# Hybrid attention layer: the last two row tiles of each projection group computed weight by weight as one

## The chip, the cores and the metric

The kernel runs as one program on one core of a Trainium2 chip. The metric is the device time of one execution in microseconds (us). Before the change the median of three runs was 1129.72 us (1129.55 to 1129.81).

## The reference

One decoder layer over 1024 rows of width 1024, in float32:

```
h = x + W_out( concat[ A heads | B heads ] )      # both read RMSNorm(x) @ W_in
y = h + W_down( relu(W_up @ RMSNorm(h))^2 )
```

- A heads: 8 query heads on 2 key/value heads of 64, a sliding window of 128 in banded blocks (128 queries against up to 256 keys), ALiBi slopes, a sink logit for each head, normalised queries and keys.
- B heads (forgetting attention): 8 heads of 64, causal, with logit[t,s] += c[t] - c[s], where c is the running sum of log sigmoid of a gate; normalised queries and keys.
- The MLP widens to 4096.

Every large product is computed in three passes on a high and a low part of each operand (hi*hi + hi*lo + lo*hi), so one tile of a projection is 8 weight blocks x 3 = 24 matmuls of 128x384 (or 128x392).

## The kernel before, in words

The program has four stages: a first projection (group A0, until 41.3 us), the attention (41.3 to 467.4 us), the up projection and the down projection. The change touches only the attention.

**Projections.** Five groups of 8 row tiles run during the attention: A1 (queries of the A heads, and the gates) and P0 to P3 (queries, keys and values of one pair of B heads each). `load_w` (L203) brings the 8 weight blocks of a group: a DMA into `wr` (3 buffers), a cast to `wh` on ScalarE, a subtraction into `wl` on GpSimd (8 buffers each of `wh` and `wl`). A buffer is free for the next group's block k when the last row tile of the group has used block k. `proj` (L216) computes one row tile into one PSUM bank of the pool `pd`, which has two banks, so that row tiles alternate. A ScalarE copy then empties the bank into `qkb` (L582) or `q` (L415), and after every fourth tile (every second in A1) `qknorm` normalises on GpSimd, VectorE and ScalarE.

**Attention units.** There are 16 A units (2 key/value heads x 8 blocks, `heads_a`) and 32 B units (4 pairs x 2 heads x 4 blocks of 256 queries, `heads_b`). A unit's scores are issued first and its mixing (transposes `tpa`/`tpb`, the split of these into `pth` on ScalarE and `ptl` on VectorE, the products `pv`/`pvb` with the values) two units later (`DEPTH`). Each unit appends its last score matmul to `marks`; "mark n" below is the last score matmul of unit n.

**Order.** Projection tiles, and later the first half of the output projection (`out_first`, matmuls `po`), are fillers: `PACE` says after how many marks each is released, and its first matmuls are put behind that mark on TensorE (`paced`). A scheduler then fixes each engine's order when the program is built: attention work has the higher priority, the splits of weights and the copies out of `pd` the highest. On the chip every engine works through its queue in that order. All loads and stores shown below are issued from SyncE's queue.

**Preparation of the next pair.** `ahead(p, u)` issues, after unit u of the 8 before pair p: at u = 4 the queries (`prep_q`: transposes, ScalarE and VectorE splits into `q1b`), at u = 5 the keys of head 0 (`prep_k`: transposes, two casts `k1b` on ScalarE and a subtraction `k2z` on VectorE for each half, one load of the gate sums `cb`), at u = 6 the values, at u = 7 the keys of head 1.

**Hand-over to the output projection.** `out_start` closes the pools of the projections, opens new ones in their place and loads the mixed heads (`mix`, 1 MB each). So its loads wait for the last projection matmul of P3. `split_mix` (SPLITS) reads a pair's mixed rows back (`mixr`), normalises and splits them; it has one buffer of each kind.

Of the kernel before, what the change touches and what calls it, by code (L numbers as in the profile page):

```python
# [8 lines left out]
F32 = mybir.dt.float32  # L9
# [3 lines left out]
ALU = mybir.AluOpType  # L13
# [3 lines left out]
P = 128  # L17
D = 1024
S = 1024
KT = D // P  # L20
NT = S // P
# [9 lines left out]
HPO = 8000  # L31
HPA = 5000
# [6 lines left out]
ORDER_END = (1, 3, 0, 2)  # L39

PACE = (
# [5 lines left out]
)  # L47

SPLITS = ((0, 4), (0, 7), (1, 1), (1, 4), (1, 6), (2, 5), (3, 5))
# [4 lines left out]
def hybrid_layer(  # L54
# [13 lines left out]
    nc = tc.nc  # L68

    def mm(out, lhsT, rhs, start, stop):  # L70
        return nc.tensor.matmul(out, lhsT, rhs, start=start, stop=stop)  # L71
# [8 lines left out]
    def rsqrt(pool, out, t, shape, tag):  # L80
# [15 lines left out]
        out=ident, in_=ident, pattern=[[-1, P]], compare_op=ALU.not_equal,  # L96
# [10 lines left out]
    ga, gm, vec, bfb, snk = (  # L107
        vt[:, a:b] for a, b in ((0, 8), (8, 16), (16, 20), (20, 28), (28, 36))
    )
# [3 lines left out]
    for i in range(2):  # L113
        nc.vector.tensor_tensor(
            out=gqk[:, i : i + 1], in0=vec[:, 2 * i : 2 * i + 1],
            in1=vec[:, 2 * i + 1 : 2 * i + 2], op=ALU.mult,
# [3 lines left out]
    rstd = cp.tile([P, NT], F32, name="rstd")  # L120
    ep2 = cp.tile([P, NT], F32, name="ep2")
    rqk = cp.tile([P, NT, 6], F32, name="rqk")
# [14 lines left out]
    xh = xg_p.tile([P, KT, S], F32R, name="xh")  # L137
    xl = xg_p.tile([P, KT, S], F32R, name="xl")
# [7 lines left out]
        out=maskd, in_=maskd, pattern=[[-1, P]], compare_op=ALU.is_ge,  # L146
# [21 lines left out]
    for k in range(KT):  # L168
# [6 lines left out]
        for cs in halves:  # L175
            nc.scalar.activation(xh[:, k, cs], xr[:, cs], AF.Copy, scale=ga[:, k : k + 1])
            nc.vector.scalar_tensor_tensor(
                out=xl[:, k, cs], in0=xr[:, cs], scalar=ga[:, k : k + 1],
                in1=xh[:, k, cs].bitcast(F32), op0=ALU.mult, op1=ALU.subtract,
# [21 lines left out]
    pd = psd.enter_context(tc.tile_pool(name="pd", bufs=2, space=PSUM, reuse_waits="tile"))  # L201

    def load_w(src, n):  # L203
        his, los = [], []
        for k in range(KT):
            wr, wh, wl = w_tiles()
            nc.sync.dma_start(wr[:, :n], src[:, k, :])
            with tc.high_priority(offset=HPO):
                split(wh[:, :n], wl[:, :n], wr[:, :n], nc.scalar, nc.gpsimd)
            his.append(wh)  # L210
            los.append(wl)
        return his, los

    middle = []

    def proj(w, n, t):  # L216
        his, los = w
        ps = pd.tile([P, 512], F32, tag="pd", name="ps")
        tsl = slice(t * P, (t + 1) * P)
        for k in range(KT):  # L220
            mm(ps[:, :n], xh[:, k, tsl], his[k][:, :n], k == 0, False)
            mm(ps[:, :n], xh[:, k, tsl], los[k][:, :n], False, False)
            pe = mm(ps[:, :n], xl[:, k, tsl], his[k][:, :n], False, k == KT - 1)
            if k == KT // 2:
                middle.append(pe.ins)
        return ps

    def qknorm(x, nh, tlo, thi, r=None):


        n = thi - tlo
        w = nh * HD
        sq = ap2.tile([P, 1024], F32, tag="sq", name="sq", bufs=1)
        sqv = sq[:, : n * w].rearrange("p (t c) -> p t c", t=n)
        xv = x[:, tlo:thi, :w]
        nc.gpsimd.tensor_tensor(out=sqv, in0=xv, in1=xv, op=ALU.mult)
        ss, r0, u = (
            ap2.tile([P, 16], F32, tag=tag, name=tag, bufs=2)[:, : n * nh]
            for tag in ("ss", "sr0", "su")
        )  # L240
        nc.vector.tensor_reduce(
            out=ss, in_=sq[:, : n * w].rearrange("p (g d) -> p g d", d=HD),
            axis=AX.X, op=ALU.add,
        )
        th = lambda a: a.rearrange("p (t h) -> p t h", h=nh)
        nc.vector.scalar_tensor_tensor(
            out=th(ss), in0=th(ss), scalar=1.0 / HD,
            in1=ep2[:, tlo:thi].unsqueeze(2).to_broadcast([P, n, nh]),
            op0=ALU.mult, op1=ALU.add,
        )  # L250
        nc.scalar.activation(r0, ss, AF.Ln)
        nc.scalar.activation(r0, r0, AF.Exp, scale=-0.5)
        nc.vector.tensor_tensor(out=u, in0=r0, in1=r0, op=ALU.mult)
        nc.vector.tensor_tensor(out=u, in0=u, in1=ss, op=ALU.mult)
        na = nh + (2 if r is not None else 0)
        if r is None:
            rv = ap2.tile([P, 16], F32, tag="r", name="r", bufs=2)[:, : n * nh]
            rv = th(rv)
        else:
            rv = r[:, tlo:thi, :]  # L260
        nc.vector.scalar_tensor_tensor(
            out=rv[:, :, :nh], in0=th(u), scalar=3.0, in1=th(r0),
            op0=ALU.subtract, op1=ALU.mult,
        )
        for t in range(n):
            xt = x[:, tlo + t, : na * HD].rearrange("p (h d) -> p h d", d=HD)
            nc.gpsimd.tensor_tensor(
                out=xt, in0=xt, in1=rv[:, t].unsqueeze(2).to_broadcast([P, na, HD]), op=ALU.mult
            )

    def split_v(src, name):
        v = ap1.tile([P, NT, P], F32R, tag="v", name=name, bufs=2)
        nc.vector.tensor_copy(v[:, :, :HD], src)
        nc.gpsimd.tensor_tensor(
            out=v[:, :, HD:], in0=src, in1=v[:, :, :HD].bitcast(F32), op=ALU.subtract
        )
        return v
# [17 lines left out]
    def paced():  # L295
        return tc.issue_after(marks[-1]) if marks else nullcontext()
# [4 lines left out]
    def tiles_q_a(g, c):  # L301
        for j in range(2):
            qa[g, j, c] = ap2.tile([P, 2, 512], F32R, tag="q1", name=f"q1a{g}{j}", bufs=4)
# [62 lines left out]
    wa1 = load_w(w_a1, 392)  # L366
    rt = cp.tile([P, NT], F32, name="rt")
    for t in range(NT):
# [4 lines left out]
        out=rt, in0=rt, scalar1=1.0 / D, scalar2=EPS, op0=ALU.mult, op1=ALU.add  # L373
# [4 lines left out]
    q3 = qk_t("q3")  # L378
    z = ap2.tile([P, NH, NT], F32, name="z")
    for t in range(0, NT, 4):  # L380
# [8 lines left out]
        out=dist, in_=dist, pattern=[[-1, 256]], compare_op=ALU.is_ge, fill=BIG,  # L389
# [3 lines left out]
        out=dist, in_=dist, pattern=[[1, 256]], compare_op=ALU.is_ge, fill=BIG,  # L393
# [7 lines left out]
    for pattern, base, sign in (  # L401
# [5 lines left out]
            out=before, in_=before, pattern=pattern, compare_op=ALU.is_ge, fill=0.0,  # L407
            base=base, channel_multiplier=sign,
        )

    def wa1_tile(t):
        with paced():
            ps = proj(wa1, 392, t)
        with tc.high_priority(offset=HPA):
            nc.scalar.copy(q3[:, t, :], ps[:, :384])  # L415
            nc.vector.scalar_tensor_tensor(
                out=z[:, :, t], in0=ps[:, 384:392], scalar=rstd[:, t : t + 1], in1=bfb,
                op0=ALU.mult, op1=ALU.add,
            )
            if t % 2:  # L420
                qknorm(q3, 6, t - 1, t + 1)

    def forget_gates():
        zf = z.rearrange("p h t -> p (h t)")
# [39 lines left out]
    def start_a():  # L464
        for c in range(2):
            tiles_q_a(0, c)
        for t in range(2):
            wa1_tile(t)
        for c in range(2):
            wa1_tile(2 + c)  # L470
            with tc.issue_after(middle[-1]):
                prep(make_k_a, q0, P, c)
            prep(make_q_a, 0, c, 0)
        for g in range(2):
            va.append(split_v(q0[:, :, 256 + g * HD : 256 + (g + 1) * HD], f"va{g}"))
        prep(make_q_a, 0, 0, 1)
        for t in range(4, NT):
            wa1_tile(t)
        prep(make_q_a, 0, 1, 1)

    def scores_a(g, i):
# [89 lines left out]
    def project_b(p):  # L571
        got = {}

        def tile_t(t):
            if t == 0:
                got["w"] = load_w(w_b[p], 384)
                qkb[p] = qk_t(f"qkb{p}")
            qk = qkb[p]
            with paced():
                ps = proj(got["w"], 384, t)  # L580
            with tc.high_priority(offset=HPO):
                nc.scalar.copy(qk[:, t, :], ps[:, :384])  # L582
            if t % 4 == 3:
                with tc.high_priority(offset=HPA):
                    qknorm(qk, 4, t - 3, t + 1, rqk)

        return [lambda t=t: tile_t(t) for t in range(NT)]

    heads = {}

# [99 lines left out]
    def prep(f, *a):  # L690
        with tc.high_priority(offset=HPA):
            return f(*a)
# [16 lines left out]
    def ahead(p, u):  # L709
        if p > 3:  # L710
            return
        if u == 4:
            prep(prep_q, p)
        if u == 5:
            prep(prep_k, p, 0)
        if u == 6:
            prep(prep_v, p, 0)
        if u == 7:
            prep(prep_k, p, 1)
# [113 lines left out]
    for dt in (0, 4):  # L833
        w = out_weights(dt, 4)

        ps = first_banks() if dt == 0 else [
            pa.tile([P, 512], F32, tag="sc", name=f"po{c}", bufs=2) for c in range(2)
        ]
# [80 lines left out]
    for dt in (1, 5, 2, 6, 3, 7):  # L919
        w = out_weights(dt, 4)  # L920
        ps = [bank(f"po{c}") for c in range(2)]
# [267 lines left out]
    for i in range(len(STEPS)):  # L1189
        down(i)  # L1190
        if STEPS[i][0] == len(PHASES) - 1 and late:
            name, dt, cs = late.pop(0)
# [63 lines left out]
```

## Time and profile before

| | |
|---|---|
| median of 3 runs | 1129.72 us |
| the profiled execution | 1130.36 us, span of its instructions 1128.5 us |
| TensorE | 1101.8 us busy, 98% of the span |
| VectorE, ScalarE, GpSimd | 770.2, 574.7, 362.0 us busy |
| mean granted clock of TensorE | 0.998 |

PE is TensorE's matmul row, PEld its weight load, DVE VectorE, ACT ScalarE, POOL GpSimd, SPq SyncE's queue. A matmul's end is modelled, so PE's busy time overstates how full it is; a gap in it is time in which nothing was in the array.

### The profile page before, as it was taken

The numbers are of one execution on the slowest core, as the hardware profiler recorded it, in microseconds if no ns is written. First come the engines' busy times: TensorE is split into PE (matmuls) and PEld (weight loads), VectorE is DVE, ScalarE is ACT, GpSimd is POOL, SyncE is SP. The second block draws the span as 40 slices with busy tenths as digits, with TensorE's granted clock in tenths as the row PEclk, the third lists the DMA queues.
The fourth block names the chain that finished last, engine by engine and source line by source line (L and its number), as shares of the span: only waits on it lengthen the run. The fifth ranks groups of instructions, "written<-read, shape, count | busy, mean of one in ns | idle before, by whom it ended". The sixth has DMA issues, their size and how long they took to land.

```text
span 1128.5 us, 15553 instructions
## 1 busy us (share of the span) xinstructions
PE 1101.8 (98%) x5551; PEld 938.8 (83%) x5551; DVE 770.2 (68%) x1311; ACT 574.7 (51%) x1013; POOL 362.0 (32%) x338
## 2 busy tenths in 40 slices
PE   9999999989999999999999999999999999999998
PEld 8999988779898887777888887888888888888886
DVE  7476665756567577799868576865574886683395
ACT  5567557757567666555454545334444433333331
POOL 5661613335323644214232332322221222222100
PEclk9999999999999999999999999999999999999999
DMA  9311301245307647373554543334699787565523
GB/s 307 127 32 40 95 15 59 87 154 174 122 26 274 222 162 248 125 247 121 196 187 177 176 169 126 145 140 168 224 391 352 265 295 263 200 229 206 185 94 112
DMA packets 95710, 195.68 MB, mean 173 GB/s; under 512 B 7136, under 2 KB 19088, under 8 KB 95632
## 3 DMA queue, kind: packets, MB, share of 16 engines
q1 hardware_dynamic: 95488, 194.66, 49.3%
q8 instruction: 44, 0.72, 0.3%
q14 instruction: 34, 0.28, 0.1%
q10 hardware_dynamic: 144, 0.02, 0.0%
HBM read 141.61 MB, written 53.04 MB: 172 GB/s over the span
## 4 chain that ended last, share of the span: by engine, by line
PE 80%; DVE 7%; DMA 5%; issue 4%; ACT 2%; POOL 2%; SPq 0%; DVEq 0%; POOLq 0%; ACTq 0%
PE pd L71 27%; PE pu L71 27%; PE ps L71 9%; PE po L71 4%; PE qps L71 3%; PE pvb L71 2%; PE spb L71 2%; DMA mixr<-mix_d 2%; PE tpb L662 2%; DMA h_d<-h 1%; PE sp L71 1%; DVE ptl L360 1%; DVE sb L626 1%; PE pv L71 1%; PE tpa L519 1%
## 5 line engine op out<-in xcount | busy, mean ns | idle before, releaser
L71 PE MATMUL pd<-hx,wx 128*128 128x512 f32 x1344 | 304.9, 389 | 0.0
L71 PEld LDWEIGHTS pd<-hx,wx 128*128 128x128 f32 x1344 | 252.4, 188 | 52.4
L71 PE MATMUL pu<-bh,wu 128*128 128x512 f32 x896 | 281.6, 395 | 1.2 <-ACT wu L75 1.2
L71 PEld LDWEIGHTS pu<-bh,wu 128*128 128x128 f32 x896 | 168.6, 188 | 41.5 <-ACT wu L75 1.6
L71 PE MATMUL pu<-bl,wu 128*128 128x512 f32 x448 | 177.0, 395 | 0.5 <-DVE bl L78 0.5
L75 ACT CAST hx<-hr 128x1024 fp32r<-128x1024 f32 x56 | 59.0, 1054 | 176.2 <-PE pd L71 171.6
L78 POOL TENSOR_TENSOR wx<-wda,wx 128x1024 fp32r<-128x1024 f32 x24 | 64.4, 2685 | 197.1 <-ACT wx L75 188.7
L78 DVE TENSOR_TENSOR hx<-hr,hx 128x1024 fp32r<-128x1024 f32 x56 | 72.8, 1307 | 73.4 <-ACT hx L75 73.4
L71 PE MATMUL ps<-wh,xh 128*128 128x384 f32 (+1 forms) x320 | 110.2, 345 | 0.3 <-ACT qkb L582 0.3
L71 PE MATMUL ps<-wh,xl 128*128 128x384 f32 (+1 forms) x320 | 109.1, 341 | 0.0
L71 PE MATMUL ps<-wl,xh 128*128 128x384 f32 (+1 forms) x320 | 109.1, 341 | 0.0
L71 PEld LDWEIGHTS pu<-bl,wu 128*128 128x128 f32 x448 | 84.3, 188 | 21.5 <-DVE bl L78 1.0
L71 PE MATMUL po<-mix,wos 128*128 128x512 f32 x384 | 96.0, 397 | 2.0 <-ACT mix L75 1.7
L78 POOL TENSOR_TENSOR wu<-wus,wu 128x512 fp32r<-128x512 f32 x32 | 48.6, 1521 | 132.2 <-ACT wu L75 132.2
L71 PEld LDWEIGHTS po<-mix,wos 128*128 128x128 f32 x384 | 69.8, 188 | 16.3 <-ACT mix L75 2.1
L75 ACT CAST wu<-wus 128x512 fp32r<-128x512 f32 x64 | 39.0, 618 | 77.6 <-PE pu L71 74.2
L78 POOL TENSOR_TENSOR wu<-wur,wu 128x512 fp32r<-128x512 f32 x32 | 43.9, 1372 | 88.7 <-ACT wu L75 88.7
L78 POOL TENSOR_TENSOR wl<-wr,wh 128x384 fp32r<-128x384 f32 (+1 forms) x47 | 50.0, 1079 | 49.7 <-ACT wh L75 37.5
L934 DVE TENSOR_TENSOR ht<-hb 128x512 f32<-128x512 f32 x32 | 21.8, 722 | 64.6 <-ACT hb L989 64.6
L360 DVE TENSOR_TENSOR ptl<-tpb,pth 128x512 fp32r<-128x512 f32 (+1 forms) x80 | 50.3, 633 | 22.0 <-ACT pth L359 20.8
L75 ACT CAST wx<-wda 128x1024 fp32r<-128x1024 f32 x56 | 58.3, 1044 | 7.3 <-DMA wda<-in_w_d_dram 7.0
L71 PEld LDWEIGHTS ps<-wh,xh 128*128 128x128 f32 x320 | 60.5, 189 | 0.8 <-ACT qkb L582 0.6
(218 smaller groups left out, 2068.7 us busy)
## 6 DMA issues: line engine op xcount, KB each, us to landing
wda<-in_w_d_dram SPq DMA_DIRECT2D x34, 1024.0 KB, 9.0
hr<-hid_d SPq DMA_DIRECT2D x56, 512.0 KB, 6.1
wur<-in_w_u_dram SPq DMA_DIRECT2D x32, 512.0 KB, 4.3
hid_d<-ht SPq DMA_DIRECT2D x16, 1024.0 KB, 4.3
hid_d<-hb SPq DMA_DIRECT2D x16, 768.0 KB, 3.7
mixs_d<-mixs SPq DMA_DIRECT2D x14, 512.0 KB, 3.4
mix<-mixs_d SPq DMA_DIRECT2D x7, 1024.0 KB, 7.4
wr<-in_w_b_dram SPq DMA_DIRECT2D x32, 192.0 KB, 2.6
```

What stands on the lines that cost most here:

```text
L71: return nc.tensor.matmul(out, lhsT, rhs, start=start, stop=stop)
L75: hi_eng.copy(hi, src)
L78: lo_eng.tensor_tensor(out=lo, in0=src, in1=hi.bitcast(F32), op=ALU.subtract)
L360: nc.vector.tensor_tensor(out=lo[:, cols], in0=pt[:, cols], in1=hi[:, cols].bitcast(F32), op=ALU.subtract)
L519: nc.tensor.transpose(tp[:, hh * P : (hh + 1) * P], pts[hh // 2][:, hh % 2, c0 : c0 + P], ident)
L626: nc.vector.tensor_tensor_reduce(out=pr[:, c * 512 : c * 512 + n], in0=sp[:, :n], in1=cb[:, c * 512 : c * 512 + n], scale=1.0, scalar=3e38 ...
L662: nc.tensor.transpose(tp[:, c0 : c0 + P], probs[qi][:, kb * P : (kb + 1) * P], ident)
L934: eng.tensor_tensor(out=out, in0=a, in1=b, op=ALU.subtract)
```

## The change

Three edits. `proj` takes several row tiles and loops over them inside the loop over weight blocks; the last two row tiles of A1 and of each of P0 to P3 are one such call (48 matmuls, two banks), and their copies follow together. `PACE` is rewritten: the pair of a group stands at the entry of tile 6 and an empty filler at that of tile 7; P0 to P3 are released at marks 2 to 8, 9 to 15, 18 to 24 and 26 to 32 (before: 2 to 9, 10 to 17, 19 to 26, 27 to 34), and the eight output tiles at 34, 36, 38, 39, 41, 42, 44, 46 (before: 36, 38, 39, 41, 42, 43, 45, 46). For pair 0 alone, `prep_q` is issued after A unit u = 3 and `prep_k` of head 0 after u = 4.

```diff
 PACE = (
-    2, 3, 4, 5, 6, 7, 8, 9,
-    10, 11, 12, 13, 14, 15, 16, 17,
-    19, 20, 21, 22, 23, 24, 25, 26,
-    27, 28, 29, 30, 31, 32, 33, 34,
-    36, 38, 39, 41, 42, 43, 45, 46,
+    2, 3, 4, 5, 6, 7, 8, 8,
+    9, 10, 11, 12, 13, 14, 15, 15,
+    18, 19, 20, 21, 22, 23, 24, 24,
+    26, 27, 28, 29, 30, 31, 32, 32,
+    34, 36, 38, 39, 41, 42, 44, 46,
 )
...
-    def proj(w, n, t):
+    def proj(w, n, *ts):
         his, los = w
-        ps = pd.tile([P, 512], F32, tag="pd", name="ps")
-        tsl = slice(t * P, (t + 1) * P)
+        pss = [pd.tile([P, 512], F32, tag="pd", name="ps") for t in ts]
         for k in range(KT):
-            mm(ps[:, :n], xh[:, k, tsl], his[k][:, :n], k == 0, False)
-            mm(ps[:, :n], xh[:, k, tsl], los[k][:, :n], False, False)
-            pe = mm(ps[:, :n], xl[:, k, tsl], his[k][:, :n], False, k == KT - 1)
+            for ps, t in zip(pss, ts):
+                tsl = slice(t * P, (t + 1) * P)
+                mm(ps[:, :n], xh[:, k, tsl], his[k][:, :n], k == 0, False)
+                mm(ps[:, :n], xh[:, k, tsl], los[k][:, :n], False, False)
+                pe = mm(ps[:, :n], xl[:, k, tsl], his[k][:, :n], False, k == KT - 1)
...
-        for t in range(4, NT):
-            wa1_tile(t)
+        for ts in ((4,), (5,), (6, 7)):
+            wa1_tiles(*ts)
...
-        return [lambda t=t: tile_t(t) for t in range(NT)]
+        ones = [lambda t=t: tiles(t) for t in range(NT - 2)]
+        return ones + [lambda: tiles(NT - 2, NT - 1), lambda: None]
...
-        if u == 4:
+        if u == (4 if p else 3):
             prep(prep_q, p)
-        if u == 5:
+        if u == (5 if p else 4):
             prep(prep_k, p, 0)
```

## Rows read from the trace of the kernel before

**Rows 1.** The page: busy time of each engine.

```profile
PE 1101.8 (98%) x5551; PEld 938.8 (83%) x5551; DVE 770.2 (68%) x1311; ACT 574.7 (51%) x1013; POOL 362.0 (32%) x338
```

**Rows 2.** Windows: stretch; length, each engine's busy time (instructions), PEclk, DMA share.

```profile
41.30:128.00 86.70, 86.58 (x532) 85.08 (x531) 58.89 (x161) 50.03 (x138) 42.94 (x42) 1.00 0.12 35
128.00:177.50 49.50, 47.25 (x294) 43.32 (x293) 32.35 (x98) 31.95 (x94) 16.49 (x17) 1.00 0.18 54
177.50:204.00 26.50, 22.27 (x131) 18.11 (x130) 17.76 (x45) 20.84 (x48) 9.68 (x9) 1.00 0.30 89
...
239.00:253.00 14.00, 10.54 (x59) 8.74 (x58) 8.39 (x19) 6.44 (x14) 6.64 (x9) 0.88 0.46 150
...
274.30:287.00 12.70, 11.62 (x79) 10.46 (x78) 10.56 (x24) 9.62 (x23) 10.82 (x15) 1.00 0.58 182
...
342.50:359.70 17.20, 15.67 (x112) 13.06 (x111) 15.35 (x41) 13.16 (x32) 8.29 (x15) 1.00 0.95 367
359.70:467.40 107.70, 103.66 (x602) 86.58 (x601) 72.25 (x166) 66.38 (x142) 47.37 (x62) 1.00 0.56 184
```

**Rows 3.** Waits of PE, 128 to 359.7 us: total, times, longest.

```profile
PE pvb L71 <- DVE ptl L360: 3.6, 4, 1.1
PE pvb L71 <- ACT pth L359: 2.1, 1, 2.1
...
PE spb L71 <- ACT k1b L330: 1.2, 1, 1.2
...
PE ps L71 <- ACT qkb L582: 0.3, 1, 0.3
```

**Rows 4.** Timeline of PE: P1's tile 7, first and last; P2's first.

```profile
189.73 0.42 PE L71 MATMUL ps<-wh,xh 128*128 128x384 f32 x1
...
193.84 0.34 PE L71 MATMUL ps<-wh,xl 128*128 128x384 f32 x1
...
204.07 0.42 PE L71 MATMUL ps<-wh,xh 128*128 128x384 f32 x1
```

**Rows 5.** Tiles wr, wl and ps: duration min/median/max in ns, first to last start.

```profile
L75 ACT CAST wh<-wr x33: 496/512/525, 41.5 to 282.6; 128x384 fp32r<-128x384 f32 x32, 128x392 fp32r<-128x392 f32 x1
L78 POOL TENSOR_TENSOR wl<-wr,wh x33: 998/1022/1047, 43.2 to 283.4; 128x384 fp32r<-128x384 f32 x32, 128x392 fp32r<-128x392 f32 x1
L582 ACT COPY qkb<-ps x32: 457/480/486, 92.5 to 343.0; 128x384 f32<-128x384 f32 x32
```

**Rows 6.** Timeline of ACT: first three casts of P2's weights, last cast.

```profile
191.76 1.34 ACT L75 CAST wh<-wr 128x384 fp32r<-128x384 f32 x3
...
204.12 0.51 ACT L75 CAST wh<-wr 128x384 fp32r<-128x384 f32 x1
```

**Rows 7.** Tiles ptq and ptk, 140 to 205 us: preparation of pair 0.

```profile
L280 ACT ACTIVATE q1b<-ptq,gqk x4: 672/684/686, 175.7 to 183.7; 64x512 fp32r<-64x512 f32 x4
...
L329 ACT CAST k1b<-ptk x4: 563/572/579, 186.7 to 202.4; 64x512 fp32r<-64x512 f32 x4
```

**Rows 8.** Timeline of PE: mark 23, P2's tile 4 end, the hole, tile 5.

```profile
233.40 0.23 PE L71 MATMUL spb<-mask_b,ident_b 128*128 128x128 bf16 x1
...
243.30 0.33 PE L71 MATMUL ps<-wh,xl 128*128 128x384 f32 x1
...
248.71 0.39 PE L71 MATMUL pvb<-pth,vb 128*128 128x256 f32 x1 [2.13 <-ACT pth L359]
...
252.23 0.59 PE L71 MATMUL ps<-wh,xh 128*128 128x384 f32 x1
```

**Rows 9.** Chain of waits in the same stretch: start, length, what.

```profile
242.31 4.18 DMA mixr<-mix_d
```

**Rows 10.** Windows around the end of that hole; columns as in rows 2.

```profile
249.00:252.60 3.60, 3.60 (x15) 2.60 (x15) 2.33 (x10) 2.32 (x5) 2.04 (x6) 0.53 0.81 279
```

**Rows 11.** Timeline of SP: first load of mixed heads.

```profile
342.58 0.38 SPq L779 DMA_DIRECT2D mix<-mixs_d  x1
```

**Rows 12.** Timeline of PE: first output matmuls.

```profile
359.72 0.94 PE L71 MATMUL po<-mix,wos 128*128 128x512 f32 x3
```

More of the change, by code (lines that the diff above doesn't have):

```diff
@@ L214, in hybrid_layer @@
     middle = []
-    def proj(w, n, t):
+    def proj(w, n, *ts):
         his, los = w
-        ps = pd.tile([P, 512], F32, tag="pd", name="ps")
-        tsl = slice(t * P, (t + 1) * P)
+        pss = [pd.tile([P, 512], F32, tag="pd", name="ps") for t in ts]
         for k in range(KT):
-            mm(ps[:, :n], xh[:, k, tsl], his[k][:, :n], k == 0, False)
-            mm(ps[:, :n], xh[:, k, tsl], los[k][:, :n], False, False)
-            pe = mm(ps[:, :n], xl[:, k, tsl], his[k][:, :n], False, k == KT - 1)
+            for ps, t in zip(pss, ts):
[3 more added lines that the diff above has]
+                pe = mm(ps[:, :n], xl[:, k, tsl], his[k][:, :n], False, k == KT - 1)
             if k == KT // 2:
                 middle.append(pe.ins)
-        return ps
+        return pss
     def qknorm(x, nh, tlo, thi, r=None):
@@ L409, in hybrid_layer, with wa1_tiles @@
         )
-    def wa1_tile(t):
+    def wa1_tiles(*ts):
         with paced():
[L413 to L421, printed above, removed]
+            pss = proj(wa1, 392, *ts)
+        for t, ps in zip(ts, pss):
+            with tc.high_priority(offset=HPA):
+                nc.scalar.copy(q3[:, t, :], ps[:, :384])
+                nc.vector.scalar_tensor_tensor(
+                    out=z[:, :, t], in0=ps[:, 384:392], scalar=rstd[:, t : t + 1], in1=bfb,
+                    op0=ALU.mult, op1=ALU.add,
+                )
+                if t % 2:
+                    qknorm(q3, 6, t - 1, t + 1)
     def forget_gates():
@@ L467, in start_a @@
         for t in range(2):
-            wa1_tile(t)
+            wa1_tiles(t)
         for c in range(2):
-            wa1_tile(2 + c)
+            wa1_tiles(2 + c)
             with tc.issue_after(middle[-1]):
@@ L476, in start_a @@
         prep(make_q_a, 0, 0, 1)
-        for t in range(4, NT):
-            wa1_tile(t)
+        for ts in ((4,), (5,), (6, 7)):
+            wa1_tiles(*ts)
         prep(make_q_a, 0, 1, 1)
@@ L572, in project_b, with tiles @@
         got = {}
-        def tile_t(t):
-            if t == 0:
+        def tiles(*ts):
+            if ts[0] == 0:
                 got["w"] = load_w(w_b[p], 384)
@@ L579, in tile_t @@
             with paced():
[L580 to L585, printed above, removed]
-        return [lambda t=t: tile_t(t) for t in range(NT)]
+                pss = proj(got["w"], 384, *ts)
+            for t, ps in zip(ts, pss):
+                with tc.high_priority(offset=HPO):
+                    nc.scalar.copy(qk[:, t, :], ps[:, :384])
+                if t % 4 == 3:
+                    with tc.high_priority(offset=HPA):
+                        qknorm(qk, 4, t - 3, t + 1, rqk)
+        ones = [lambda t=t: tiles(t) for t in range(NT - 2)]
+        return ones + [lambda: tiles(NT - 2, NT - 1), lambda: None]
     heads = {}
```

## The prediction

> **What bounds the kernel now.** I read the page's busy times first. TensorE is in use 98% of the span and no other engine above 68% [rows 1], so the kernel's time is TensorE's work plus the gaps in it. The change leaves the number and the shapes of the matmuls as they are; it can only move gaps. So the second view was the table of windows [rows 2]: length minus PE busy is the gap time of a stretch. Over A1 and P0 (41.3 to 128 us) it is 86.70 - 86.58 = 0.1 us: there TensorE is full, and nothing that is released sooner can end sooner. It is 49.50 - 47.25 = 2.25 us in 128 to 177.5 (P1 beside the A units), 4.23 us in 177.5 to 204 (the passage from A units to B units), 3.46 us in 239 to 253, 1.08 us in 274.3 to 287 (from P2 to P3), 1.53 us in 342.5 to 359.7 (from P3 to the output tiles) and 4.04 us in the rest of the attention, which the edits hardly reach. The third view, PE's waits [rows 3], says what ends these gaps: the evictions of transposes (`ptl` 3.6 us, `pth` 2.1 us), the first keys of pair 0 (`k1b` 1.2 us), and only once, for 0.3 us, a copy out of a projection bank. No row has TensorE waiting for `wh` or `wl`. Late weights therefore cost nothing directly; they cost because no projection matmul can stand in the gaps while the next group is not there.
>
> **The change, part by part.**
>
> *Weight by weight.* A row tile's 24 matmuls take 193.84 - 189.73 = 4.1 us when nothing stands between them [rows 4], a pair 8.2 us. Block k of the group is now given up between 1 and 8 us after the start of the pair, instead of between 0.5 and 4 us after the start of the last tile: the first one about 3.6 us sooner, counted from the end of the group. The refill itself, 8 casts of 0.51 us on ACT, 8 subtractions of 1.02 us on POOL [rows 5] and the loads between, took from 191.76 to past 204.12 us for P2 [rows 6], some 13 us; it is longer than the pair, so nearly all of the 3.6 us arrives at its end. Where this is worth something: from P2 to P3, gap 1.08 us [rows 2]. I take 0.5 us (bounds 0 and 1.08). From P1 to P2 the weights came while the pace held P2 back (its first matmul stands at 204.07 [rows 4]), so there the pace decides. On SP, the loads of blocks 3 to 7 still wait for POOL's subtractions and stores of mixed rows queue behind them; these stores are read much later, so I put nothing on that.
>
> *Two banks at once.* The pair needs both banks of `pd`. Its second tile starts three matmuls after its first and waits for the copy of the tile before (0.48 us [rows 5]); the next group's first tile waits for the pair's first copy, which begins only three matmuls before the pair's end. That is two new waits at each of five groups. Behind such a waiting matmul stand all later attention matmuls, for TensorE works in order. Mostly other work lies between: ten microseconds from P1 to P2 [rows 4]. Bounds: nothing, and 10 x 0.48 = 4.8 us; I take 0.5 us, one of the ten, nearest to the single 0.3 us that the copy costs now [rows 3].
>
> *Pace, P1.* Every tile of P1 is released one mark sooner, so that at each gap of 128 to 177.5 us a tile is at hand. Into the same stretch come pair 0's queries and first keys: four splits of 0.68 us on ACT [rows 7], as many on VectorE, four casts of 0.57 us at most, 16 transposes and one load; ACT is busy 31.95 of 49.5 us and VectorE 32.35 [rows 2], which covers them. Of 2.25 us I take 1.3. Bounds: all of the 2.25, and a loss of 2.7 us (the ACT splits uncovered).
>
> *Passage from A to B.* P1 now ends with the pair at mark 15, so units 16 and 17 have no projection beside them until P2's first tile at mark 18; before, tile 6 stood at mark 16, tile 7 at mark 17 (189.73) and P2's first tile at mark 19 (204.07) [rows 4]. Against the lost filler stands a shorter chain: ACT, busy 20.84 of 26.5 us here [rows 2], loses 4 x 0.68 us of query splits, 2 x 0.57 us and more of first keys and most of 8 x 0.51 us of weight casts, and the wait for `k1b` (1.2 us [rows 3]) should go. Bounds: the whole 4.23 us gained, or 5.8 us lost (below, in the fourth rival). I take 0.7 us of gain, near the middle but on the side of the shorter ACT.
>
> *The hole of 239 to 253 us.* P2's tile 4 ends at 243.30, tile 5 is held by mark 24 and starts at 252.23; between them TensorE stood for 2.13 us before one product alone [rows 8]. ACT and VectorE had stopped behind the read-back of mixed rows, a load that landed only 4.18 us after 242.31 [rows 9]. After it the granted clock stood at 0.53 for 3.6 us [rows 10], the lower level of 1.2 GHz for most of it: 3.6 x (1 - 0.53) = 1.7 us more. So the hole costs 3.46 + 1.7 = 5.2 us. With the change tile 5 is released at mark 23, which was at 233.40 [rows 8], and 4.1 us of matmuls can lie in the hole. They help where the scheduler puts them before the blocked product, and not behind it. Bounds 0 and 5.2 us; I take about half, 2.5 us.
>
> *P3 and the output tiles.* The loads of mixed heads start with P3's last matmul (342.58 [rows 11]) and the first output matmul came 17.1 us later (359.72 [rows 12]), with DMA engines 95% busy [rows 2]. P3 ends sooner and so the same 17 us come sooner, beside other units; mark 34 for the first output tile can't be met. I put 0, between a gain and a loss of 1.5 us, the gap time of that stretch. A1's pair and P0's earlier end lie in the full stretch: nothing.
>
> **Sum.** 1.3 + 0.7 + 2.5 + 0.5 - 0.5 = 4.5 us. The profiled execution took 1130.36 us, 1.86 us more than its span; 1130.36 - 4.5 = 1125.9. The median of the runs lies 0.64 us under the profiled execution, so I predict 1125.2 us (its own range 1122.5 to 1127.4).
>
> **The rivals.**
>
> 1. *The passage is freed as well.* If the earlier queries and keys take the whole of the 4.23 us and not 0.7, the time is 1125.2 - 3.5 = 1121.7. For it: ACT's load there falls by a third. Against: two units with no filler.
>
> 2. *The gaps only change place.* Each of the waits is for an eviction [rows 3], not for a weight; the queue order is written by a planner which does not know when a load lands, and a shifted filler may uncover as many gaps as it fills. Then 1129.7. For it: most single gaps are about 1 us. Against: the big hole has a cause that the pace touches.
>
> 3. *The banks bind.* All ten waits of the pair are paid: 4.8 us in place of 0.5, so 1125.2 + 4.3 = 1129.5. For it: tiles follow each other closely where TensorE is full. Against: that full stretch has attention matmuls to put between, and the copies have the highest priority. The Trainium skill, Perfetto Trace Analysis, section Matmuls, says that independent matmul groups should rotate through the PSUM banks so that one's evacuation overlaps the next one's matmuls; a pair that takes both banks breaks this rotation. By that rule the time is this rival's; the trace of before, where tiles alternate, has the one 0.3 us wait and so agrees with it.
>
> 4. *The passage starves: slower.* Place: units 16 and 17, 177.5 to 204 us. If the chain through evictions sets the pace of these units whatever ACT has lost, the 24 matmuls of tile 7 that filled 4.1 us there leave 4.1 us of gap, and a gap of that size with small matmuls around it lowers the clock as at 249 us, 1.7 us: 5.8 us together. If the hole at 239 is set by its load in any case, what is left on the other side is 1.3 + 0.5 - 0.5 = 1.3 us, and the time is 1129.7 + 5.8 - 1.3 = 1134.2. It decides from the point where more than about 4.5 us of the lost filler shows as gap. For it: the stretch had 4.23 us of gaps even with two tiles in it. Against: ACT's shorter list, and P2's first tile one mark sooner.
>
> **How the numbers follow.** Forecast 0.42, rival 1 0.18, rival 2 0.13, rival 3 0.06, rival 4 0.21. About 0.2%, 2.3 us, is what a measurement of this kernel can tell from no change. Faster: 0.42 + 0.18 = 0.60; the same: 0.13 + 0.06 = 0.19; slower: 0.21. Low end: with every bound of gain met (2.25 + 4.23 + 5.2 + 1.08 = 12.8 us) it would be 1116.9; 1119.0 leaves out the last of that. High end: 1132.5, short of rival 4's full price, which leaves about a tenth out above.
>
> **What would show it.** Right: windows over P1 and over the units around P2's tile 5 with under 1 us of gap each and a granted clock of 1.00 there; no wait of over 1 us for `k1b`; the casts of P2's and P3's weights done before the group's first matmul. Wrong: waits of `ps` for `qkb` or `q` adding up to microseconds (rival 3); over 7 us of gap or a granted clock under 1 between the pair of P1 and P2's first tile (rival 4); the five gaps named above, 12.6 us in all, come back in other places (rival 2).

## The result and the profile after

The changed kernel takes 1134.49 us (median of 22 runs, 1130.30 to 1136.83); beside it the kernel before took 1129.68 us (22 runs, 1128.48 to 1133.41). The ratio is 1.0036, interval 1.0028 to 1.0044: slower by more than the 0.2% that can be told here, where I had forecast 4.5 us of gain. The profiled execution took 1133.83 us; its span is 1131.7 us with a mean granted clock of 0.994, against 1128.5 us and 0.998 before. One run each of `e4_p0_single` (1813 us), of `e7_read_later` (1511 us) and of the kernel before beside it (1817 us) was slow throughout; the medians and ratios here leave these out.

The page's busy row of the changed kernel, which answers to [rows 1], shows the same matmuls and 2.2 us more of busy TensorE:

```profile
PE 1104.0 (98%) x5551; PEld 942.2 (83%) x5551; DVE 767.3 (68%) x1311; ACT 576.1 (51%) x1013; POOL 358.7 (32%) x338
```

Busy time grows without more matmuls when the clock is lower. So each stretch is read twice: length minus PE busy is gap, length times (1 - PEclk) is time lost to the clock. The windows of the changed kernel, columns as in [rows 2], at the same places in the program:

```profile
41.10:128.50 87.40, 87.07 (x532) 85.20 (x530) 61.05 (x162) 49.69 (x137) 43.09 (x42) 1.00 0.11 30
128.50:178.50 50.00, 45.53 (x279) 42.95 (x278) 30.53 (x90) 32.37 (x89) 16.35 (x16) 0.97 0.19 60
178.50:205.20 26.70, 23.98 (x136) 20.25 (x135) 17.98 (x53) 20.84 (x53) 13.87 (x14) 0.94 0.33 99
...
240.00:257.00 17.00, 14.99 (x100) 13.82 (x100) 11.82 (x25) 9.94 (x23) 8.07 (x12) 1.00 0.46 152
257.00:275.00 18.00, 16.97 (x113) 15.72 (x112) 8.87 (x24) 12.97 (x30) 13.05 (x14) 1.00 0.69 208
275.00:288.00 13.00, 12.82 (x86) 11.79 (x84) 8.92 (x20) 8.20 (x19) 7.09 (x11) 1.00 0.33 112
288.00:336.50 48.50, 48.05 (x316) 45.38 (x316) 30.97 (x78) 29.15 (x64) 12.49 (x22) 1.00 0.24 80
336.50:354.80 18.30, 16.04 (x104) 13.13 (x102) 13.63 (x35) 13.53 (x31) 6.57 (x12) 0.91 0.83 323
354.80:470.40 115.60, 109.85 (x642) 91.83 (x642) 73.91 (x183) 72.01 (x154) 49.08 (x67) 1.00 0.53 175
```

The row of the kernel before for P3's own stretch:

```profile
287.00:342.50 55.50, 54.05 (x358) 51.13 (x357) 30.95 (x79) 32.22 (x72) 14.93 (x24) 1.00 0.19 62
```

The same view of the changed kernel, around the three places where the clock fell; the lower value is 0.50, which is 1.2 GHz:

```profile
128.50:132.60 4.10, 0.98 (x8) 0.61 (x6) 0.43 (x2) 1.51 (x4) 1.43 (x2) 1.00 0.55 189
132.60:136.00 3.40, 3.36 (x10) 3.36 (x11) 0.69 (x1) 2.02 (x5) 3.40 (x4) 0.50 0.46 129
...
194.00:197.50 3.50, 3.50 (x14) 2.88 (x14) 3.38 (x8) 3.06 (x12) 3.15 (x3) 0.51 0.69 207
...
344.20:347.60 3.40, 3.40 (x16) 2.90 (x15) 1.86 (x7) 1.78 (x5) 1.36 (x2) 0.50 1.02 410
```

Each of the last three rows costs at most 3.4 x (1 - 0.50) = 1.7 us. The kernel before had one such stretch [rows 10]. With gap and clock added, before and after:

| stretch | before: gap + clock | after: gap + clock | change | forecast |
|---|---|---|---|---|
| P1 beside the A units | 2.25 + 0 | 4.47 + 1.7 | +3.9 | -1.3 |
| passage A to B | 4.23 + 0 | 2.72 + 1.7 | +0.2 | -0.7 |
| the hole at P2's tile 5 | 3.46 + 1.7 | 2.01 + 0 | -3.2 | -2.5 |
| 257 to 288 us, with P2 to P3 | 1.08 + 0 | 1.21 + 0 | +0.1 | -0.5 |
| P3's own, until its end | 1.45 + 0 | 0.45 + 0 | -1.0 | 0 |
| P3 to the output tiles | 1.53 + 0 | 2.26 + 1.7 | +2.4 | 0 |
| output tiles to the attention's end | 4.04 + 0 | 5.75 + 0 | +1.7 | 0 |

(The 0.5 us that I had put for the banks has no stretch of its own.) The seven come to +4.2 us before rounding; the spans differ by 3.2. The clock is what is counted too high: two more stretches at the lower clock would be 3.4 us, and TensorE's busy time grew by 2.2 us only, so 1.7 us each is an upper reading. The gaps of all seven together grew from 18.0 to 18.9 us. The hole gained about what was forecast. From P2 to P3 the gap of 1.08 us is down to 0.18, but the 18 us before it, where the kernel before had none, now have 1.03. The largest loss is in P1's stretch, and the waits of PE from 128.5 to 354.8 us (total, times, longest; they answer to [rows 3]) put it in one place:

```profile
PE ps L71 <- ACT qkb L587: 3.5, 2, 3.2
PE pvb L71 <- DVE ptl L363: 2.7, 4, 1.9
PE pvb L71 <- ACT pth L362: 2.1, 2, 1.1
PE pv L71 <- ACT pth L362: 1.3, 2, 1.0
PE tpa L523 <- DVE k2z L335: 0.9, 1, 0.9
...
```

TensorE waited once for 3.2 us, for a copy out of a projection bank that takes under half a microsecond [rows 5]. The timeline of PE shows it as the first matmul of P1:

```profile
128.82 0.66 PE L523 MATMUL tpa<-ident,sa 128*128 128x128 f32 x4
132.64 0.69 PE L71 MATMUL ps<-wh,xh 128*128 128x384 f32 x1 [3.16 <-ACT qkb L587]
```

What ScalarE did meanwhile, in its timeline (in brackets: idle time before, and what ended it):

```profile
123.21 1.56 ACT L75 CAST wh<-wr 128x384 fp32r<-128x384 f32 x3 [0.94 <-PE ps L71]
130.54 0.51 ACT L75 CAST wh<-wr 128x384 fp32r<-128x384 f32 x1 [5.77 <-DMA wr<-in_w_b_dram]
131.57 0.51 ACT L75 CAST wh<-wr 128x384 fp32r<-128x384 f32 x1 [0.52 <-DMA wr<-in_w_b_dram]
132.11 0.86 ACT L587 COPY qkb<-ps 128x384 f32<-128x384 f32 x2
132.85 0.52 ACT L75 CAST wh<-wr 128x384 fp32r<-128x384 f32 x1
133.27 0.60 ACT L362 CAST pth<-tpa 128x512 fp32r<-128x512 f32 x1
```

P0's pair gave up its first weight blocks while it was still running, so the casts of P1's blocks stand in ScalarE's queue ahead of the pair's two copies. There are three raw buffers `wr`, three casts went through, and the fourth waited 5.77 us for its load. Both copies stood behind it and the fifth, both banks were full, P1's first matmul needed one, and the attention's matmuls stood behind that one. The chain of waits tells why the load was late (start, length, what; pieces of under 0.1 us between these are left out):

```profile
124.18 0.43 DVE mta L534
124.62 2.34 DMA mix_d<-mta
127.02 0.32 SPq L566
127.44 0.38 SPq L207
127.86 3.63 DMA wr<-in_w_b_dram
131.57 0.45 ACT wh L75
132.11 0.49 ACT qkb L587
132.64 4.07 PE ps L71 x13
```

On SP's queue the weight load (L207) stands behind the read-back of mixed rows (L566), which waits until the store of these rows has landed. The Trainium skill, PSUM — Partial Sum Buffer, section Engine vs sequencer instructions, says that the queues of ScalarE, VectorE and GpSimd are strict first in, first out. The trace agrees: the copies at 132.11 begin when the casts before them end.

The kernel before has the same order on ScalarE in small, and I had not read these two lines:

```profile
128.64 0.51 ACT L75 CAST wh<-wr 128x384 fp32r<-128x384 f32 x1 [2.48 <-DMA wr<-in_w_b_dram]
129.06 0.47 ACT L582 COPY qkb<-ps 128x384 f32<-128x384 f32 x1
```

There too a cast stood for its load, 2.48 us, and the copy of P0's last tile stood behind it. It cost nothing because the tile before had been copied ahead of the casts, so that one bank was free.

### The profile page after: what moved, and what is told of

It is laid out like the page before. It is cut to its first block, busy times and chain, and to the rows that moved or that the text cites. A ratio compares the mean times of both kernels' runs of the same rounds, so it can differ in the third digit from the quotient of the medians.

```text
span 1131.7 us, 15569 instructions
## 1 busy us (share of the span) xinstructions
PE 1104.0 (98%) x5551; PEld 942.2 (83%) x5551; DVE 767.3 (68%) x1311; ACT 576.1 (51%) x1013; POOL 358.7 (32%) x338
## 4 chain that ended last, share of the span: by engine, by line
PE 77%; DVE 9%; DMA 6%; ACT 3%; issue 2%; POOL 2%; SPq 0%; DVEq 0%; ACTq 0%; POOLq 0%
PE pd L71 27%; PE pu L71 26%; PE ps L71 9%; PE po L71 4%; PE spb L71 2%; PE pvb L71 2%; PE tpb L668 2%; DVE ptl L363 1%; DMA mixr<-mix_d 1%; PE sp L71 1%; PE pv L71 1%; PE tpa L523 1%; DMA xq<-in_x_dram 1%; DMA xr<-in_xT_dram 1%; ACT pth L362 1%
```

## The experiments

Three theories. *Cast theory*: the loss at P0's end needs the pair and the casts ahead of its copies. *Bank theory* (rival 3): two full banks are enough, whatever stands ahead. *Passage theory* (rival 4): the lost filler at units 16 and 17 is what costs. All ratios are against the kernel before, run beside; its medians there were 1129.66 to 1130.75 us, so gains and losses below are taken from the ratios where nothing else is said. By its ratio the whole change costs 0.0036, 4.1 us.

| kernel | median us | ratio | interval | clock at its lower level near (us, profile) |
|---|---|---|---|---|
| e4_p0_single | 1129.66 | 0.9995 | 0.9985 to 1.0006 | 338 |
| e5_copy_dve | 1129.79 | 1.0001 | 0.9991 to 1.0010 | 250, 342 |
| e8_no_pairs | 1129.08 | 0.9986 | 0.9976 to 0.9996 | 342 |
| e1_pairs_only | 1138.52 | 1.0078 | 1.0066 to 1.0091 | 133, 249, 279 |
| e9_five_raw | 1130.89 | 1.0008 | 0.9994 to 1.0021 | 190, 248 |
| e7_read_later | 1131.03 | 1.0016 | 1.0003 to 1.0029 | none |
| e2_pace_only | 1133.94 | 1.0038 | 1.0025 to 1.0050 | 193, 432 |
| e12_pairs_only_five | 1136.92 | 1.0064 | 1.0047 to 1.0082 | 200, 255 |
| e3_prep_only | 1132.34 | 1.0013 | 1.0005 to 1.0022 | 250 |
| e13_pairs_pace | 1134.88 | 1.0034 | 1.0022 to 1.0046 | 132, 196, 254 |
| e11_no_pairs_five | 1129.13 | 0.9989 | 0.9979 to 1.0000 | 190, 340 |
| e14_no_pairs_later | 1128.90 | 0.9984 | 0.9969 to 0.9998 | 189, 247 |

**P0's last two tiles one after the other again**, all else as changed:

```
     def project_b(p):
...
+        if p == 0:
+            return [lambda t=t: tiles(t) for t in range(NT)]
         ones = [lambda t=t: tiles(t) for t in range(NT - 2)]
```

> The changed kernel with P0's tiles 6 and 7 as two single tiles (both still released at mark 8); pairs in A1, P1, P2, P3; pace and early preparation as changed. Bank theory: P1's first tile finds a bank free, no wait for a copy there, clock 1.00 at 128 to 137 us, time about 1129.5 (5 us under the changed kernel). Passage theory: about 1134.5 within 1.5.

Measured 1129.66 us: from 1.0036 to 0.9995 is 4.6 us, so the whole loss lies with this one pair of the five. Its ScalarE timeline, over the same stretch as above:

```profile
123.75 0.48 ACT L587 COPY qkb<-ps 128x384 f32<-128x384 f32 x1 [2.17 <-PE ps L71]
124.28 1.68 ACT L75 CAST wh<-wr 128x384 fp32r<-128x384 f32 x3
130.43 0.51 ACT L75 CAST wh<-wr 128x384 fp32r<-128x384 f32 x1 [4.48 <-DMA wr<-in_w_b_dram]
130.85 0.47 ACT L587 COPY qkb<-ps 128x384 f32<-128x384 f32 x1
```

ScalarE stands for 4.48 us here too. But tile 6 was copied at 123.75, before the casts, so one bank was free for P1. The window 126 to 137 us has 11.00 - 10.38 = 0.6 us of gap, as much as in the kernel before, and the full clock; the changed kernel has 3.2 us of gap there and a clock of 0.84:

```profile
126.00:137.00 11.00, 10.38 (x64) 9.29 (x63) 5.10 (x16) 5.55 (x18) 7.61 (x7) 1.00 0.51 166
```

**The pairs stay, the copies of those of P0 to P3 go to VectorE:**

```
-                    nc.scalar.copy(qk[:, t, :], ps[:, :384])
+                    if len(ts) > 1:
+                        nc.vector.tensor_copy(qk[:, t, :], ps[:, :384])
+                    else:
+                        nc.scalar.copy(qk[:, t, :], ps[:, :384])
```

> The changed kernel with one edit: the two copies out of the projection banks that follow a pair of P0 to P3 run on VectorE instead of ScalarE. Bank theory (TensorE stood 3.2 us before P1's first tile because the pair holds both banks and its copies stood on ScalarE behind casts of weights that had not landed; then 3.4 us at half clock, 1.7 us; 5 us together): the wait of ps for qkb falls under 0.5 us, the granted clock stays 1.00 from 128 to 137 us, and the time falls from 1134.5 to about 1129.5. Passage theory (the loss lies in the units between P1's pair and P2's first tile, which have no projection beside them): the wait goes as well, but the time stays within 1.5 us of 1134.5, with gaps and a half clock near 194 us.

Measured 1129.79 us, ratio 1.0001: 4.0 us come back. ScalarE's wait there, and the window 126 to 137 us:

```profile
ACT wh L75 <- DMA wr<-in_w_b_dram: 7.9, 3, 6.0
```

```profile
126.00:137.00 11.00, 10.02 (x60) 8.46 (x59) 5.62 (x17) 5.70 (x17) 6.74 (x6) 1.00 0.58 183
```

The cast waits as long as ever (6.0 us), but no copy stands behind it: the window has 1.0 us of gap, against 0.6 before, and the full clock. The late load by itself costs little.

**Five raw weight buffers in place of three**, pairs and copies as changed:

```
-            for tag, dt, n in (("wr", F32, 3), ("wh", F32R, 8), ("wl", F32R, 8))
+            for tag, dt, n in (("wr", F32, 5), ("wh", F32R, 8), ("wl", F32R, 8))
```

> The changed kernel with five buffers of wr instead of three (pairs, pace and copies on ScalarE as changed), so that blocks 3 and 4 of the next group lie there before their casts. Bank-and-cast theory (ScalarE's queue stands on a cast whose load has not landed, and the copies stand behind it): ScalarE's wait for wr loads at 120 to 137 us, 7.7 us in the changed kernel, falls under 2 us, the wait of ps for qkb there under 1 us; time about 1129.5, 5 us under the changed kernel. Pure bank theory (holding two banks costs the wait whatever ScalarE does): wait and time as in the changed kernel, 1134.5.

Measured 1130.89 us, ratio 1.0008: 3.2 us come back. The same two views:

```profile
ACT wh L75 <- DMA wr<-in_w_b_dram: 2.2, 3, 1.2
```

```profile
126.00:137.00 11.00, 11.00 (x71) 10.52 (x70) 5.75 (x18) 7.37 (x21) 8.68 (x8) 1.00 0.73 222
```

The pair still fills both banks and TensorE has no gap at all. The bank theory falls: a pair by itself costs nothing here, it needs a blocked queue ahead of its copies.

**The read-back of mixed rows issued behind P1's last weight load on SP:**

```
+    loads = []
...
-            nc.sync.dma_start(wr[:, :n], src[:, k, :])
+            loads.append(nc.sync.dma_start(wr[:, :n], src[:, k, :]))
...
-            nc.sync.dma_start(m, mix_d[e][:, cs])
+            with tc.issue_after(loads[23].ins) if e == 0 else nullcontext():
+                nc.sync.dma_start(m, mix_d[e][:, cs])
```

> The changed kernel with one queue edit: the first read-back of mixed rows (mixr of split_mix 0) is issued behind the last of P1's weight loads on SyncE and not before the fourth. Cast theory, with SyncE's queue as part of its cause: P1's fourth block lands about 1.2 us sooner (the load is issued near 126.2 instead of 127.4), ScalarE's 5.8 us of standing and the wait of ps for qkb (3.2 us) each shrink by about 1.2 us, and the time falls by 1 to 3 us (the half clock may go or stay). If that read has no part in it: waits as in the changed kernel.

Measured 1131.03 us, ratio 1.0016: 2.3 of the 4.1 us are back (3.5 by the medians). ScalarE's longest wait for a load fell from 5.8 to 1.3 us, TensorE's for the bank from 3.2 to 0.6 us, both by more than the 1.2 us that I had expected. The fourth cast waits 3.8 us for TensorE now, until the pair has used the block that it overwrites, and both casts and copies are done by 130.4 us. So the order on SP is what made the load late. What the later read-back costs elsewhere was not separated.

**No pairs at all**, the new pace and the earlier queries and keys kept:

```
-        for ts in ((4,), (5,), (6, 7)):
+        for ts in ((4,), (5,), (6,), (7,)):
...
-        ones = [lambda t=t: tiles(t) for t in range(NT - 2)]
-        return ones + [lambda: tiles(NT - 2, NT - 1), lambda: None]
+        return [lambda t=t: tiles(t) for t in range(NT)]
```

> The changed kernel without any pair: pace and early preparation as changed, the last two tiles of every group one after the other (both released at the pair's mark). Bank theory: about 1129.5, the pace and the early preparation cost nothing. Passage theory: the loss is the pace's, so 1134.5 or above, since weights also come 3.6 us later.

Measured 1129.08 us, ratio 0.9986 with an interval that stays below 1. The earlier release of weights thus buys nothing that shows. The other four pairs cost some 0.6 us by the medians and 1.0 us by the ratios of e4 and this kernel; the intervals overlap, so this is not resolved.

**The pairs alone**, on the kernel before, with its pace and its preparation (the changed kernel with the `PACE` table and the two lines of `ahead` put back):

> The kernel before with the pairs alone: pace as before (the pair stands where tile 6 stood, at marks 8, 16, 25, 33, nothing where tile 7 stood) and preparation as before. Bank theory: P1's first tile is held by mark 10 until the copies are done, so the pair costs little: 1129.7, between 1128.5 and 1131. If the pair is bad wherever it stands (each group's start waits for copies), 1132 or more. Passage theory: with the old pace, 1129.7 or less.

Measured 1138.52 us, worse than the whole change. The windows show a loss at P0's end (126 to 137 us) and the clock at 239 to 257 us and 257 to 288 us:

```profile
126.00:137.00 11.00, 7.55 (x40) 7.01 (x39) 5.58 (x17) 6.05 (x19) 6.71 (x6) 0.84 0.54 182
...
239.00:257.00 18.00, 13.99 (x77) 12.45 (x76) 10.94 (x22) 8.98 (x18) 8.60 (x12) 0.81 0.37 120
257.00:288.00 31.00, 28.60 (x166) 26.75 (x165) 16.28 (x36) 18.36 (x41) 16.63 (x18) 0.89 0.52 165
```

The first costs 3.45 us of gap and 11 x 0.16 = 1.8 us of clock. TensorE did not wait for the bank there but 3.4 us for a `pth` split, which stood on ScalarE behind the two copies and these behind a cast that waited 5.6 us for its load. The other two lose 18 x 0.19 + 31 x 0.11 = 6.8 us to the clock, behind single waits of 4.0 us for `ptl` and 1.9 us for a copy (`qkb`). With the old pace the pairs thus cost more, and in other places too.

**The same with five raw buffers** (the edit of e9 on e1):

> The kernel before with the pairs alone (the earlier run of this came to 1138.5) and five buffers of wr. Cast theory: ScalarE's 5.7 us of standing before P1's fourth cast goes, with the 3.4 us of pv behind it and the half clock after; 1138.5 falls by 4 us or more, to 1134 or less. If the pairs' loss there comes from somewhere else (the pace against the pairs), it stays above 1136.

Measured 1136.92 us, more than I expected. ScalarE's longest wait for a load at P0's end fell from 5.6 to 1.0 us, but only 1.6 us came back, with intervals that overlap. The rest stands elsewhere: 18.00 - 12.92 = 5.1 us of gap at 239 to 257 us, 2.95 us at 137 to 178 us. Why the pairs with the old pace open these gaps was not settled.

**The new pace alone**, on the kernel before (its `PACE` table only):

> The kernel before with the new pace alone: single tiles, preparation of pair 0 as before. Cast theory: no loss, 1128 to 1130, like the run without pairs (1129.1). Passage theory, in the form that the early preparation is what saved that run: above 1131.

Measured 1133.94 us, 4.3 us lost; by the cast theory I had expected about nothing, and the passage theory was right here in kind. The longest wait and the window of the passage:

```profile
PE tpa L519 <- DVE k2z L332: 2.3, 2, 2.1
```

```profile
178.00:206.00 28.00, 22.68 (x126) 18.71 (x124) 17.51 (x48) 20.60 (x49) 13.10 (x13) 0.94 0.31 94
```

It has 5.3 us of gap and 28 x 0.06 = 1.7 us of clock; the kernel before has 4.2 us there and the full clock. In the same window e8, which differs by the earlier queries and keys, has 3.3 us of gap and the full clock:

```profile
178.00:206.00 28.00, 24.66 (x151) 20.86 (x150) 20.00 (x56) 22.83 (x58) 13.84 (x14) 1.00 0.32 94
```

So the passage starves if tile 7 leaves it and nothing else does: rival 4's mechanism is real, at 1.1 us of gap and 1.7 us of clock where it had put 4.1 and 1.7. The earlier preparation pays for it. The rest of e2's loss stands behind P3: from 354.8 to 470 us it has 5.99 us of gap against 4.28 before, and one more stretch at the lower clock.

**The earlier queries and keys alone**, on the kernel before:

```
-        if u == 4:
+        if u == (4 if p else 3):
...
-        if u == 5:
+        if u == (5 if p else 4):
```

> The kernel before with the early preparation of pair 0 alone (single tiles, old pace). Passage theory, as far as the pace alone (1133.9) and the pace with the preparation (1129.1) show it: the early preparation shortens the chain between the A and the B units, so with the old pace it gains too, up to the 3.4 us of gaps at 182 to 188 us: 1127 to 1129. If it is only the pace's cure and worth nothing by itself: 1129 to 1131. If it loads ScalarE and VectorE beside the A units: above 1131.

Measured 1132.34 us, the case that I had put last. The passage did gain: its gap from 178 to 206 us went from 4.23 to 3.49 us. But A1 and P0 (41.3 to 128 us) went from 0.12 to 1.07 us of gap (new waits of 0.6 us for `z` and 0.4 us for `q1a`, both on VectorE) and 137 to 178 us from 1.63 to 2.73 us. With the old pace the gap changes place, and 1.5 us are lost.

**The change without that preparation** (pairs and new pace):

> The changed kernel without the early preparation (pairs and new pace). If the losses add up (pairs some 5 us, pace without the preparation some 4 us above the kernel before), 1139. If the pace covers what the pairs lose (P1's first tile at hand for the gap), 1134 to 1136.

Measured 1134.88 us. Pace alone costs 4.3 us and P0's pair 4.6 us, yet the two together cost no more than the whole change. The parts do not add; the scheduler writes a new order for each kernel.

**No pairs, five raw buffers**, and **no pairs, later read-back** (the edits of e9 and e7 on e8):

> No pairs, new pace, early preparation, five buffers of wr. Cast theory: where no copy stands behind a blocked cast, more raw blocks are worth little: 1128 to 1129.5, about as without them (1129.1). If ScalarE's standing on weight casts costs the single tiles as well: 1127 or less.

> No pairs, new pace, early preparation, and the first read-back of mixed rows issued behind P1's weight loads. Cast theory: the fourth cast stands 1.2 us less; no copy waits behind it in this order, so 1128 to 1129.5; a gain to under 1128 would say that the read-back's place costs the single tiles too.

Measured 1129.13 and 1128.90 us, ratios 0.9989 and 0.9984: not to be told from e8's 0.9986. As far as these runs can tell, raw buffers and the order on SP matter only where a pair waits behind them. e14 has the lowest ratio of all, 0.16% under the kernel before; it is the change without its pairs and with the later read-back.

## Why the prediction was wrong

I forecast 1125.2 us; 1134.49 us lies above my range, and above rival 4's 1134.2 us, which had come to nearly this time by another way.

- *Two banks at once: 0.5 us, "one of the ten, nearest to the single 0.3 us that the copy costs now".* This is the step that failed. Nine of the ten waits cost 0.3 us together, less than I put; the tenth cost 3.2 us and then 1.7 us of clock. My upper bound, ten times 0.48 us, took the copy's length for the price of a wait. The price is the time until ScalarE reaches the copy. The evidence against rival 3, that the copies have the highest priority, did not hold: the casts have the same one, and they ran first. The trace of before had shown a copy standing behind a cast that waited 2.48 us. Shown by three edits that each take one link away: tiles single (e4), copies on another queue (e5), loads in time (e9).
- *SP: "I put nothing on that".* I looked at stores queued behind weight loads. What mattered was the reverse: weight loads behind a read-back that waits for a store. e7 moves that alone and brings back 2.3 us.
- *Weight by weight: 0.5 us.* From P2 to P3 the gap fell by 0.9 us, and 1.0 us came back just before it. Over both (257 to 288 us) e8, without pairs, has 2.46 us of gap against 1.21 in the changed kernel, but e9, with pairs, has 2.44, and e8 is no slower than the kernels with them. In the time the release was worth nothing that shows, as my own reading of the waits said (no row waits for weights), and at P0's end it put the casts ahead of the copies: 123.21 us, against 124.28 in e4.
- *Pace, P1: 1.3 us.* Without the one wait the stretch has 4.47 - 3.2 = 1.3 us of gap against 2.25: a gain of 1.0 us. The kernels with the new pace that lack the long wait have 1.1 to 2.0 us in 128 to 178 us, so the gain is some 0.3 to 1.15 us: right in kind, and smaller than I put.
- *Passage: 0.7 us.* The gap fell by 1.5 us and the clock took 1.7 us. ScalarE's shorter list, which was to pay for the lost filler, did not come about: it was busy 20.84 us in this stretch before and 20.84 us after, since two query splits and two casts of keys left it, but eight casts of weights in place of seven and more of the A units' work stood in it. e2 shows the starving that I priced in rival 4, e8 shows it paid by the earlier preparation.
- *The hole: 2.5 us.* It gained 3.2 us: 1.45 us of gap and the 1.7 us of clock. Tile 5 did move ahead of the blocked product, which still waited 1.95 us. The clock's part was in some measure luck: from 239 to 257 us e14, e5 and e9 have 2.04 to 2.32 us of gap, the changed kernel 2.01, and in those three the clock fell there again (0.91).
- *P3 to the output tiles: 0.* P3 ended 6 us sooner and the first output matmul came 4.9 us sooner, as forecast, but the stretch took 0.7 us more of gap and 1.7 us of clock. The drop there also stands in e4, e5, e8 and e11 (338 to 342 us), not in e2, e7, e9, e13 and e14; its cause was not tested.
- *"the rest of the attention, which the edits hardly reach": nothing.* This term, with the 0 for P3 to the output tiles, was wrong as well. Without the pair only half of the 9 us between forecast and result comes back: e4 has the gains in P1, the passage and the hole (gaps of 1.83, 3.01 and 2.46 us, all at the full clock), and yet it is no faster than the kernel before. From 336.5 to 470 us the kernel before has 5.8 us of gap; the kernels with the old pace have 4.4 to 5.6, e4 has 7.8 and every kernel with the new pace 6.8 to 8.3 us (one execution each). P3 ends 6 us sooner and no longer fills gaps there; that this is the cause was not tested by itself.
- *The sum.* The gaps came out as rival 2 says: those of the five stretches were 12.6 us before and 12.7 us after. Rival 2 had no term for the clock. The low end of the range, 1119.0, does not follow from its words (12.8 - 1.08 us gives 1118.0); nothing hangs on it.

Of the marks I had named, P2's casts were done before its first matmul, no wait for `k1b` over 1 us was left and the hole had its full clock. The gaps of P1 and of the hole did not fall under 1 us (4.47 and 2.01), and P3's last cast (272.93 us) came after its first matmul (271.88). The mark of rival 3 was met (waits of `ps` for `qkb` in microseconds), and that of rival 4 through the clock in the passage, not through its gap. The Trainium skill's rule cited in the prediction (Perfetto Trace Analysis, section Matmuls: rotate independent groups through the banks so that one's evacuation overlaps the next one's matmuls) pointed the right way. The runs agree with it only in part: in e9 a pair fills both banks and TensorE has no gap from 126 to 137 us, so what was lost is decided by the queue ahead of the evacuation.

## What to carry to other kernels

When a change lets two results wait in all the banks there are, price that wait by what stands before the evacuation in its engine's queue, and follow that instruction to the load it waits for, and the load to what stands before it on its own queue. An earlier release is a gain only where something waits for it; where nothing does, it only moves work forward in a queue, ahead of something that is waited for. And read the gaps and the granted clock of a stretch together, since the gaps of 3.2 us at 129 us here and of 3.5 us in the hole before were paid up to half as much again in the matmuls that followed.

## What the runs showed of the hardware

After the 3.2 us gap at 129 us the granted clock was 0.50 for 3.4 us, and 0.50 or 0.51 for as long at 194 and 344 us, where the gaps just before were several of 0.2 to 1.1 us. In e1 two such stretches lasted 6.8 us, in e13 one. Gaps of the same size did not always bring one: from 239 to 257 us the changed kernel had 2.01 us of gap at the full clock, e14 had 2.04 us with such a stretch. How many there are differs between kernels that differ little (none in e7's profile, one in e4's, three in the changed kernel's), and the time follows: over the 22 runs of the changed kernel the mean granted clock was 0.9948, over 27 runs of the kernel before 0.9976. If TensorE is busy throughout, 0.0028 x 1131 us = 3.2 us of the 4.8 us between the medians is clock rather than gap; that is an upper reading, and the two profiled executions show 2.2 us of it as longer busy time. It may also be why the parts of this change do not add: an edit that moves gaps can add or take away such a stretch, worth up to 1.7 us either way. That was not tested by itself.
